# Finer hand-over between dense products and a latency chain in a decoder block: three delays and the place of a yield

## The chip, the cores and the metric

One core of a Trainium2 chip runs one launch of the kernel. The metric is the device time of that launch in microseconds: 951.49 us as the median of three runs before the change (948.81 to 954.71). A second, profiled execution took 951.66 us; all rows below are from it.

## The reference, cut to what matters

A decoder block on 512 tokens of 1024 channels. One normed input feeds one wide projection; its columns go to two branches, which a gate merges, and a feed-forward part follows.

```
xn = rms_norm(h, mix_norm);  proj = xn @ w_in
# attention branch: 8 heads of 64; a small "indexer" picks 128 keys for each query
scores = sum_h relu(q_idx[h] . k_idx / 8) * w_idx[h];  sel = top_k(scores, 128)
y_attn = softmax(rms(q) . rms(k)[sel] / 8 + rel_bias) @ v[sel]
# recurrent branch (RWKV-7): a linear recurrence over time with 8 states of 64 x 64
state = state * d_t + (state @ -kk_t) b_t + v_t k_t ;  y_t = state @ r_t
y = group_norm(y) * ln_w + ln_b + sum(r * k * r_k) * v     # the last term: the "bonus"
merged = sigmoid(gate_attn) * (y_attn @ w_a) + sigmoid(gate_rwkv) * (y_rwkv @ w_r)
h = h + merged @ w_out
h = h + (silu(hn @ w_gate) * (hn @ w_up)) @ w_down,   hn = rms_norm(h, ffn_norm)
```

All tensors are float32.

## The kernel before, in words

**Dense products.** Every weight product is split: a weight chunk is rounded to a high part (`w_hi`, ScalarE, L239) and the rest is a low part (`w_lo`, GpSimd, or VectorE for every third chunk, L243); activations are split in the same way. Three TensorE products, hi by hi, hi by lo and lo by hi, make one step of the sum (`dense_t`, L255 to L264). These are the tiles `ps_d` of the profile. They wait for little, and there is always a next one, until the program's own list of them is at a point that needs a branch's result.

**Chains.** Between the dense products the kernel puts the latency-bound work: index scores (`scores`), the choice of 128 keys by 16 rounds of max and match-replace on VectorE (`select`), head norms (`queries`, `keys`, `key_norms`, each asking TensorE for sums of squares by `head_sums`), attention (`attention`, 4 query tiles by 8 heads, in units of one head: flip the weights of the head two units back, logits of this head, values of the head three back), the operands of the recurrence (`prepare`, `operands`, with a small product for the bonus, L714), the triangular inverses of its four 128-token tiles (`invert`), its eight chunk steps (`steps`) and `head_norm`.

**What sets the order.** TensorE's order is written out while the program is built, by the class `Streams`: each piece of work is a generator with a rank, and a clock `now` that adds an assumed time for each product. At every `yield` the generator says how long after now it wants to go on (or which signal it waits for), and the piece of the lowest rank that is due goes next; the dense products have the highest rank number and fill what is left. The delays stand in the table `L` (L89). Nothing on the chip looks at that clock: the order is fixed, and where a delay was too short TensorE, which works in order, stands and waits. VectorE, ScalarE, GpSimd and the DMA queue of SyncE get their order from a scheduler that follows TensorE's.

The pieces and delays that the change touches: `dense_t` yields once for three products; `L["sums"]` stands between a square of a head tile on ScalarE and its sum on TensorE (L489, L512, L687); `L["attn"]` has one delay for each query tile, after each attention unit (L550); `L["bonus"]` stands between the GpSimd product `ag` (L709) and its sum on TensorE (L719). The point where the dense list needs the recurrence is `yield "yr"` (L1045): the products of `yr` follow it.

Of the kernel before, what the change touches and what calls it, by code (L numbers as in the profile page):

```python
# [82 lines left out]
for _n, _c in _PARS:  # L83
# [2 lines left out]

L = dict(norm=3.0, normed=1.3, score=0.4, pick=0.15, rms=6.5, sums=2.5, attn=(1.0, 0.6, 0.4, 0.35), attn_out=2.0, sig=0.3,  # L89
         prep=5.0, oper=6.0, bonus=6.0, mat=0.5, mats=2.8, inv_u=3.25, inv_t=1.4, inv_r=1.4, inv_n=0.9, inv_e=1.8,  # L90
         inv=1.8, vals=0.6, st_b=1.0, st_u=1.36, st_m=1.4, hn_b=4.55, hn_n=6.55, hn_g=2.0)
POOL_ONLY = 17
COPIES = 23
# [34 lines left out]
def hybrid_block(ctx: ExitStack, tc: tile.TileContext, x, first, rows, consts, lora, rel_bias, stream, out):  # L128
# [10 lines left out]
    def bank(tag, dt=F32, name=None):  # L139
        n = {"d": 3, "i": 2, "c": 3}[tag]  # L140
        return pp.tile([128, 512], dt, name=name or "ps_" + tag, tag=tag, bufs=n)
# [19 lines left out]
    def mm(o, w, r, **kw):  # L161
        nc.tensor.matmul(o, w, r, **kw)  # L162
        n = 1
        for d in r.shape[1:]:
            n *= d
        st.now += max(n * 4 / 2400, 0.107) if r.dtype == F32 else max(n / 2400, 0.03)
# [51 lines left out]
    def cst(name):  # L218
        o, e = CONST_AT[name]
        return con[:, o:e]  # L220
# [34 lines left out]
    def dense_t(ps, wt, c, act, t0=0, t1=S):  # L255

        k = len(act)
        for j in range(k):
            xh, xl = act[j][0][:, t0:t1], act[j][1][:, t0:t1]
            hi, lo = wt[j][0][:, c], wt[j][1][:, c]  # L260
            mm(ps, hi, xh, start=(j == 0), stop=False)
            mm(ps, hi, xl, start=False, stop=False)
            mm(ps, lo, xh, start=False, stop=(j == k - 1))
            yield 0.0  # L264

# [36 lines left out]
    def dense_halves(outs, act, name):  # L302

        for t in (0, 2):
            yield f"{name}{t}"
            yield f"{name}{t + 1}"
            for ps, wt in outs:
                yield from dense_t(ps[:, t * 128:t * 128 + 256], wt, slice(0, 128), act, t * 128, t * 128 + 256)
# [6 lines left out]
    def norm(t, src, gain, to, name):  # L315
# [11 lines left out]
        for g in range(2):  # L327
            nc.vector.scalar_tensor_tensor(xs[g], src[g], ss[:, 3:4], gain[g], op0=OP.mult, op1=OP.mult)
        yield L["norm"]
        ts = slice(t * 128, t * 128 + 128)  # L330
        for g in range(2):
# [4 lines left out]
            nc.vector.tensor_sub(to[1][g][:, :, ts], ps, to[0][g][:, :, ts])  # L336
        st.signal(f"{name}{t}", L["normed"])

# [70 lines left out]
    def scores():  # L409
        for i in range(1, NT):  # L410
            n = (i + 1) * 128
            sc = unit("score")[:, :n]
            for h in range(H):
# [7 lines left out]
                else:  # L421
                    r = unit("relu")[:, :n]
                    nc.scalar.activation(r, ps, AF.Relu)
                    nc.vector.scalar_tensor_tensor(sc, r, w, sc, op0=OP.mult, op1=OP.add)  # L424
                yield L["score"]
            nc.vector.tensor_add(sc[:, n - 128:], sc[:, n - 128:], cst("causal"))
# [3 lines left out]
    def select():  # L430
        for i in range(1, NT):
            yield f"score{i}"
            sc, n = keep[i], (i + 1) * 128
            for _ in range(TOPK // 8):
                m8 = small("max8", 8)
                nc.vector.max(m8, sc)  # L436
                nc.vector.match_replace(sc, m8, sc, TAKEN)  # L437
                yield n / 480 + L["pick"]
            nc.vector.tensor_scalar(sc, sc, CUT, NEG, op0=OP.is_gt, op1=OP.mult)
# [32 lines left out]
    def queries(j, ps):  # L472
# [5 lines left out]
        def rest():  # L478
            s = head_sums(sq)
            nc.vector.tensor_scalar(qss[:, :, 2 * j:2 * j + 2], s.rearrange("q (t h) -> q t h", h=2), RMS_EPS, None,  # L480
                                    op0=OP.add)
            if j == 3:
                flat = lambda q: q.rearrange("q t h -> q (t h)")
                nc.gpsimd.tensor_tensor(flat(qrs[:, 0]), flat(qss), half, op=OP.pow)
                nc.vector.tensor_mul(flat(qrs[:, 1]), flat(qss), flat(qrs[:, 0]))
                st.signal("q", 8.0)
            yield 0.0

        st.add(3, rest(), L["sums"])  # L489

    def keys(j, ps):
# [4 lines left out]
        def rest():  # L496
# [4 lines left out]
            nc.scalar.activation(hv(sq), rs[:, :, None].to_broadcast([128, 8, 64]), AF.Copy)  # L501
            yield L["rms"]
            ps = bank("i")
# [458 lines left out]
    def gate(dst):  # L962

        ps = bank("d")
        yield from dense_t(ps, w_tile(128), slice(0, 128), xn)
        nc.scalar.activation(dst, ps, AF.Tanh, scale=0.5)

    def gated(dst, j, wt, act):
        ps = bank("d")
        yield from dense_t(ps, wt, slice((j % 2) * 128, (j % 2) * 128 + 128), act)  # L970
        nc.vector.scalar_tensor_tensor(dst, dst, 1.0, ps, op0=OP.add, op1=OP.mult)
# [239 lines left out]
```

## Time and profile before

| what | value |
|---|---|
| median of three runs | 951.49 us |
| profiled execution | 951.66 us |
| its span, first to last instruction | 949.9 us |
| TensorE matmuls (PE) busy | 911.4 us, 96% |
| VectorE (DVE) | 406.5 us, 43% |
| ScalarE (ACT) | 344.5 us, 36% |
| GpSimd (POOL) | 365.4 us, 38% |

The chain that ended last is 79% TensorE and 11% VectorE by share of the span. The VectorE share is an average: the profile's 40 slices show it at 8 to 9 tenths in the third to eighth slice and at 1 tenth or less from the 26th on, where the feed-forward part runs on TensorE alone.

### The profile page before, as it was taken

Reading aid. Unit: us, or ns where it says so; the run is one execution under the profiler, and the core shown is the slowest. Engines: PE = TensorE matmul, PEld = TensorE weight load, DVE = VectorE, ACT = ScalarE, POOL = GpSimd, SP = SyncE. Lnnn points to the kernel's source line nnn. Section 1 sums busy time; section 2 is a strip of 40 time slices with the busy share of each in tenths; the row PEclk is TensorE's granted clock in tenths of the full one; section 3 lists DMA queues with packets and bytes.
Section 4 is the critical chain, followed back from the end, with each engine's and each line's share of the span. In section 5 each row is a group of like instructions: output and inputs, shape, how many; then the busy total and the mean of one; then the engine's idle time right before and its main releaser. Section 6 shows DMA issues by size and latency. Waiting matters only on the chain.

```text
span 949.9 us, 13573 instructions
## 1 busy us (share of the span) xinstructions
PE 911.4 (96%) x5526; PEld 765.4 (81%) x5526; DVE 406.5 (43%) x796; ACT 344.5 (36%) x548; POOL 365.4 (38%) x242
## 2 busy tenths in 40 slices
PE   7999899899989999999998999999999999999998
PEld 5988797688767777878886998888888888888886
DVE  4389898873573546573534616111111111100111
ACT  5554565543542433233423324323223232221120
POOL 6425532203264353525415632443534344432321
PEclk9999899999999999999999999999999999999999
DMA  6321232101222120201142332233232332332431
GB/s 230 92 79 44 88 117 68 45 1 59 86 67 67 46 67 23 68 20 50 46 133 79 94 94 68 89 94 106 88 111 89 99 101 90 91 108 89 138 107 44
DMA packets 24173, 77.77 MB, mean 82 GB/s; under 512 B 2869, under 2 KB 4366, under 8 KB 24112
## 3 DMA queue, kind: packets, MB, share of 16 engines
q1 hardware_dynamic: 20688, 72.49, 24.3%
q10 hardware_dynamic: 3424, 4.43, 1.7%
q8 instruction: 43, 0.70, 0.3%
q14 instruction: 18, 0.15, 0.0%
HBM read 74.53 MB, written 2.38 MB: 81 GB/s over the span
## 4 chain that ended last, share of the span: by engine, by line
PE 79%; DVE 11%; ACT 3%; POOL 3%; issue 3%; DMA 1%; SPq 0%; ACTq 0%; POOLq 0%; DVEq 0%
PE ps_d L162 57%; PE ps_c L162 11%; PE ps_i L162 9%; DVE score L437 2%; DVE max L436 2%; PE ps_c L169 2%; DVE score L424 1%; POOL w_lo L243 1%; DMA xa<-in_x_dram 1%; DVE qs L460 1%; PE ps_i L169 1%; ACT w_hi L239 1%; ACT lg L574 0%; POOL bb L700 0%; DVE w_lo L243 0%
## 5 line engine op out<-in xcount | busy, mean ns | idle before, releaser
L243 POOL TENSOR_TENSOR w_lo<-w_raw,w_hi 128x1024 fp32r<-128x1024 f32 (+1 forms) x94 | 221.1, 2354 | 366.8 <-ACT w_hi L239 360.0
L239 ACT ACTIVATE w_hi<-w_raw 128x1024 fp32r<-128x1024 f32 x129 | 136.6, 1060 | 370.9 <-PE ps_d L162 213.1
L162 PE MATMUL ps_d<-xnh,w_hi 128*128 128x512 f32 (+2 forms) x360 | 149.7, 416 | 0.0
L162 PE MATMUL ps_d<-hnl,w_hi 128*128 128x512 f32 (+1 forms) x368 | 139.9, 380 | 0.4 <-DVE hnl L336 0.4
L162 PE MATMUL ps_d<-hnh,w_hi 128*128 128x512 f32 (+1 forms) x368 | 139.9, 380 | 0.0
L162 PE MATMUL ps_d<-hnh,w_lo 128*128 128x512 f32 (+1 forms) x368 | 139.7, 380 | 0.0
L162 PE MATMUL ps_d<-xnh,w_lo 128*128 128x512 f32 (+2 forms) x360 | 137.6, 382 | 0.0
L162 PE MATMUL ps_d<-xnl,w_hi 128*128 128x512 f32 (+2 forms) x360 | 137.4, 382 | 0.0
L243 DVE TENSOR_TENSOR w_lo<-w_raw,w_hi 128x1024 fp32r<-128x1024 f32 x37 | 45.6, 1233 | 130.8 <-ACT w_hi L239 130.0
L1095 DVE TENSOR_TENSOR gsig<-ps_d,gsig 128x512 f32<-128x512 f32 x22 | 15.2, 692 | 157.6 <-PE ps_d L162 156.9
L162 PEld LDWEIGHTS ps_d<-hnl,w_hi 128*128 128x128 f32 x368 | 69.2, 188 | 13.8 <-DVE hnl L336 0.6
L162 PEld LDWEIGHTS ps_d<-hnh,w_lo 128*128 128x128 f32 x368 | 69.2, 188 | 13.1
L162 PEld LDWEIGHTS ps_d<-hnh,w_hi 128*128 128x128 f32 x368 | 69.2, 188 | 13.0
L162 PEld LDWEIGHTS ps_d<-xnh,w_lo 128*128 128x128 f32 x360 | 68.9, 191 | 13.1
L162 PEld LDWEIGHTS ps_d<-xnh,w_hi 128*128 128x128 f32 x360 | 69.4, 193 | 11.7 <-issue 2.6
L162 PEld LDWEIGHTS ps_d<-xnl,w_hi 128*128 128x128 f32 x360 | 69.4, 193 | 9.9 <-issue 1.9
L1099 POOL TENSOR_TENSOR ul<-gsig,uh 128x512 fp32r<-128x512 f32 x22 | 31.6, 1434 | 25.3 <-ACT uh L1098 25.3
L801 POOL COPY rr<-eye 128x512 f16<-128x512 f16 x20 | 13.5, 680 | 57.2 <-PE ps_i L162 57.2
L162 PE MATMUL ps_d<-w_hi,mh 128*128 128x256 f32 x120 | 34.0, 284 | 0.0
L162 PE MATMUL ps_d<-w_hi,ml 128*128 128x256 f32 x120 | 34.0, 283 | 0.0
L162 PE MATMUL ps_d<-w_lo,mh 128*128 128x256 f32 x120 | 34.0, 283 | 0.0
L574 ACT ACTIVATE lg<-lg,mx,qrs 128x128 f32<-128x128 f32 (+3 forms) x32 | 20.8, 649 | 22.1 <-DVE mx L573 22.0
(291 smaller groups left out, 1698.5 us busy)
## 6 DMA issues: line engine op xcount, KB each, us to landing
w_raw<-in_stream_dram SPq DMA_DIRECT2D x129, 512.0 KB, 3.6
xa<-in_x_dram SPq DMA_DIRECT2D x4, 512.0 KB, 5.8
ht<-in_x_dram ACTq DMA_DIRECT2D x8, 256.0 KB, 3.1
out_dram<-ht SPq DMA_DIRECT2D x8, 256.0 KB, 2.2
toep<-bias_table ACTq DMA_DIRECT2D x8, 128.0 KB, 3.4
gain<-in_rows_dram ACTq DMA_DIRECT2D x2, 256.0 KB, 3.1
con<-in_consts_dram SPq DMA_DIRECT2D x1, 321.0 KB, 6.9
bias_table<-tab ACTq DMA_DIRECT2D x1, 276.0 KB
```

The costliest lines, as they stand in the source:

```text
L162: nc.tensor.matmul(o, w, r, **kw)
L169: nc.tensor.transpose(o, src, idn)
L239: nc.scalar.activation(hi, raw, AF.Copy)
L243: eng.tensor_sub(lo[:, o:o + n_], raw[:, o:o + n_], hi[:, o:o + n_])
L424: nc.vector.scalar_tensor_tensor(sc, r, w, sc, op0=OP.mult, op1=OP.add)
L436: nc.vector.max(m8, sc)
L437: nc.vector.match_replace(sc, m8, sc, TAKEN)
L460: nc.vector.scalar_tensor_tensor(lo[b, h], src[a], gain[a], hi[a, h], op0=OP.mult, op1=OP.subtract)
L574: nc.scalar.activation(lg, lg, AF.Exp, scale=scale, bias=mx[:, 2:3], accum_out=den[:, h:h + 1])
L801: nc.gpsimd.tensor_copy(two(R, 1), eye16.rearrange("q (g w s) -> q g w s", w=2, s=s)[:, None, :, 1] .to_broadcast([128, H, 64 // s, s]))
L1095: nc.vector.tensor_mul(g, pu, g)
L1099: nc.gpsimd.tensor_sub(ul, g, uh)
```

## The change

Three numbers or groups of numbers in the table of delays change, and `dense_t` gives way behind each product instead of behind each third. `dense_k` and `dense_tiles`, the other two forms of dense product, are as before. Two lines are added to the file, so all lines behind L261 have a number higher by two in the new kernel.

```diff
-L = dict(norm=3.0, normed=1.3, score=0.4, pick=0.15, rms=6.5, sums=2.5, attn=(1.0, 0.6, 0.4, 0.35), attn_out=2.0, sig=0.3,
-         prep=5.0, oper=6.0, bonus=6.0, mat=0.5, mats=2.8, inv_u=3.25, inv_t=1.4, inv_r=1.4, inv_n=0.9, inv_e=1.8,
+L = dict(norm=3.0, normed=1.3, score=0.4, pick=0.15, rms=6.5, sums=4.0, attn=(0.9, 0.9, 0.95, 1.0), attn_out=2.0, sig=0.3,
+         prep=5.0, oper=6.0, bonus=9.0, mat=0.5, mats=2.8, inv_u=3.25, inv_t=1.4, inv_r=1.4, inv_n=0.9, inv_e=1.8,
...
             mm(ps, hi, xh, start=(j == 0), stop=False)
+            yield 0.0
             mm(ps, hi, xl, start=False, stop=False)
+            yield 0.0
             mm(ps, lo, xh, start=False, stop=(j == k - 1))
             yield 0.0
```

What it does to the order, at three places.

ScalarE, at the squares of the key tiles (`ksq<-ps_d` is the square of a tile, `ksq<-qrs` the spread of an earlier tile's norm, `kh<-kraw` the scaled keys of that earlier tile). Before:

```order
L493 ACTIVATE ksq<-ps_d 128x512
L494 ACTIVATE kraw<-ps_d,fst 128x512
L501 ACTIVATE ksq<-qrs 128x512 x2
L456 ACTIVATE kh<-kraw 64x512
L462 ACTIVATE kh<-kraw 64x512
L456 ACTIVATE kh<-kraw 64x512
L462 ACTIVATE kh<-kraw 64x512
L493 ACTIVATE ksq<-ps_d 128x512
L494 ACTIVATE kraw<-ps_d,fst 128x512
```

Now:

```order
L495 ACTIVATE ksq<-ps_d 128x512
L496 ACTIVATE kraw<-ps_d,fst 128x512
L503 ACTIVATE ksq<-qrs 128x512
L495 ACTIVATE ksq<-ps_d 128x512
L496 ACTIVATE kraw<-ps_d,fst 128x512
L503 ACTIVATE ksq<-qrs 128x512
L458 ACTIVATE kh<-kraw 64x512
L464 ACTIVATE kh<-kraw 64x512
L458 ACTIVATE kh<-kraw 64x512
L464 ACTIVATE kh<-kraw 64x512
```

The third tile's square stood behind two spreads and four scalings; it stands behind one spread now.

TensorE, in the attention of the last query tile (`lg` are the weights to flip, `kh` and `kl` the logits, `vt` the values, `ps_d` the dense products). Before:

```order
L162 MATMUL ps_c<-kh,qs 128x512
L162 MATMUL ps_c<-kl,qs 128x512
L162 MATMUL ps_i<-vt,pt 128x64 x4
L162 MATMUL ps_d<-xnh,w_hi 128x512
L162 MATMUL ps_d<-xnl,w_hi 128x512
L162 MATMUL ps_d<-xnh,w_lo 128x512
L169 MATMUL ps_c<-fst,lg 128x128 x4
L162 MATMUL ps_c<-kh,qs 128x512
L162 MATMUL ps_c<-kl,qs 128x512
L162 MATMUL ps_i<-vt,pt 128x64 x4
L169 MATMUL ps_c<-fst,ytile 128x128 x4
L169 MATMUL ps_c<-fst,lg 128x128 x4
```

Now:

```order
L162 MATMUL ps_c<-kh,qs 128x512
L162 MATMUL ps_c<-kl,qs 128x512
L162 MATMUL ps_i<-vt,pt 128x64 x4
L162 MATMUL ps_d<-xnl,w_hi 128x512
L162 MATMUL ps_d<-xnh,w_lo 128x512
L162 MATMUL ps_d<-xnh,w_hi 128x512
L162 MATMUL ps_d<-xnl,w_hi 128x512
L162 MATMUL ps_d<-xnh,w_lo 128x512
L169 MATMUL ps_c<-fst,lg 128x128 x4
L162 MATMUL ps_c<-kh,qs 128x512
L162 MATMUL ps_c<-kl,qs 128x512
L162 MATMUL ps_i<-vt,pt 128x64 x4
```

Between two units stand five dense products where three, or none, stood.

TensorE, where the dense list comes to `yr` (`zg` and `z_g` are the last head norm's products). Before:

```order
L169 MATMUL ps_d<-fst,ytok 128x128 x4
L162 MATMUL ps_d<-zg,g2a 128x128
L162 MATMUL ps_d<-z_g_128,g2b 128x128
L162 MATMUL ps_d<-zg,g2a 128x128
L162 MATMUL ps_d<-z_g_128,g2b 128x128
L162 MATMUL ps_d<-zg,g2a 128x128
L162 MATMUL ps_d<-z_g_128,g2b 128x128
L162 MATMUL ps_d<-zg,g2a 128x128
L162 MATMUL ps_d<-z_g_128,g2b 128x128
L162 MATMUL ps_d<-yr,w_hi 128x512 x2
```

Now, up to the first seven of the 60 dense products that follow:

```order
L162 MATMUL ps_d<-zg,g2a 128x128
L162 MATMUL ps_d<-z_g_128,g2b 128x128
L162 MATMUL ps_d<-zg,g2a 128x128
L162 MATMUL ps_d<-z_g_128,g2b 128x128
L162 MATMUL ps_d<-xnh,w_hi 128x512
L162 MATMUL ps_d<-xnl,w_hi 128x512
L162 MATMUL ps_d<-xnh,w_lo 128x512
L162 MATMUL ps_d<-xnh,w_hi 128x512
L162 MATMUL ps_d<-xnl,w_hi 128x512
L162 MATMUL ps_d<-xnh,w_lo 128x512
L162 MATMUL ps_d<-xnh,w_hi 128x512
```

Sixty dense products of 512 columns stand between the last head norm and the first product of `yr`, where none stood.

## Rows read from the trace of the kernel before

**Rows 1.** Busy time by stage: busy us (instructions) of each engine, granted clock, DMA.
```profile
50.00:145.00 95.00, 88.21 (x508) 77.84 (x508) 87.33 (x202) 53.63 (x88) 38.64 (x16) 0.95 0.26 79
145.00:222.00 77.00, 70.04 (x446) 59.09 (x445) 59.73 (x200) 41.66 (x97) 12.05 (x6) 0.98 0.14 44
```

**Rows 2.** TensorE's waits: tile and line, releaser, us in total, times, longest.
```profile
PE ps_c L169 <- ACT lg L574: 7.7, 10, 1.7
PE ps_i L162 <- POOL ag L709: 5.0, 3, 2.8
...
PE ps_i L162 <- ACT ksq L493: 4.3, 1, 4.3
PE ps_d L162 <- ACT yr L1048: 3.5, 1, 3.5
...
PE ps_i L162 <- ACT tt L811: 1.8, 2, 0.9
PE ps_i L162 <- DVE uu L814: 1.6, 2, 0.8
PE ps_c L162 <- DVE score L420: 1.1, 1, 1.1
```

**Rows 3.** Windows of 5 us around the lower clock (PEclk stands before DMA).
```profile
105.00:110.00 5.00, 2.67 (x10) 2.54 (x11) 4.08 (x11) 4.86 (x8) 0.38 (x1) 0.56 0.00 0
110.00:115.00 5.00, 5.00 (x25) 4.25 (x23) 3.88 (x10) 3.62 (x7) 3.60 (x2) 0.76 0.12 14
200.00:205.00 5.00, 5.00 (x26) 4.32 (x24) 3.08 (x9) 1.56 (x4) 0.80 (x1) 0.66 0.01 2
510.00:515.00 5.00, 4.78 (x13) 3.60 (x14) 2.50 (x5) 1.48 (x3) 0.00 (x0) 0.68 0.05 17
```

**Rows 4.** ScalarE's timeline at the keys: start, us, instruction, idle before.
```profile
103.58 0.63 ACT L501 ACTIVATE ksq<-qrs 128x512 f32<-128x512 f32 x1 [5.56 <-POOL qrs L500]
...
106.71 0.57 ACT L493 ACTIVATE ksq<-ps_d 128x512 f32<-128x512 f32 x1
```

**Rows 5.** Timelines of TensorE and VectorE at the first attention unit.
```profile
140.09 0.22 PE L162 MATMUL ps_c<-kh,qs 128*128 128x128 f32 x1
...
144.82 0.33 PE L169 MATMUL ps_c<-fst,lg 128*128 128x128 f32 x1 [1.38 <-ACT lg L574]
...
142.24 0.33 DVE L563 SCALAR_TENSOR_TENSOR lg<-toep,qrs,ps_c 128x128 f32<-128x128 f32 x1
...
143.34 0.68 DVE L436 MAX8 max<-score 128x8 f32<-128x512 f32 x1
```

**Rows 6.** TensorE's timeline behind a foreign product (head sums): three dense starts.
```profile
90.43 0.49 PE L162 MATMUL ps_d<-xnh,w_hi 128*128 128x512 f32 x1
90.75 0.40 PE L162 MATMUL ps_d<-xnl,w_hi 128*128 128x512 f32 x1
90.99 0.40 PE L162 MATMUL ps_d<-xnh,w_lo 128*128 128x512 f32 x1
```

**Rows 7.** GpSimd's timeline at the third bonus product.
```profile
276.43 2.37 POOL L243 TENSOR_TENSOR w_lo<-w_raw,w_hi 128x1024 fp32r<-128x1024 f32 x1 [1.25 <-ACT w_hi L239]
278.76 1.70 POOL L709 TENSOR_TENSOR ag<-zr,ag 128x512 f32<-128x512 f32 x1
```

**Rows 8.** TensorE and ScalarE timelines inside an inverse.
```profile
376.70 1.06 ACT L239 ACTIVATE w_hi<-w_raw 128x1024 fp32r<-128x1024 f32 x1 [1.30 <-PE ps_d L162]
...
382.29 0.41 PE L162 MATMUL ps_i<-rr,uu 128*128 128x64 f16 x8
...
382.80 0.60 ACT L811 ACTIVATE tt<-ps_i 128x512 f16<-128x512 f32 x1 [4.01 <-PE ps_i L162]
```

**Rows 9.** VectorE and GpSimd timelines in the index scores.
```profile
58.49 2.17 DVE L424 SCALAR_TENSOR_TENSOR score<-relu,widx,score 128x384 f32<-128x384 f32 x1
...
61.85 0.59 DVE L424 SCALAR_TENSOR_TENSOR score<-relu,widx,score 128x384 f32<-128x384 f32 x1
...
57.85 2.40 POOL L243 TENSOR_TENSOR w_lo<-w_raw,w_hi 128x1024 fp32r<-128x1024 f32 x1 [9.74 <-ACT w_hi L239]
```

## The prediction

> **What bounds the kernel now.** I read TensorE's waits first, then the busy time by stage, then the timelines around each long wait. TensorE is busy nearly all the time, so the change can only earn the stalls, and what the lower clock costs behind them. The waits [rows 2] say where the stalls are: 7.7 us in ten waits of the attention's flips for the exponentials (`lg`), 5.0 us in three waits of the bonus sums for GpSimd (`ag`), 4.3 us in one wait for the square of a key tile (`ksq`), 3.5 us in one wait for `yr`. The rest of these rows, 4.5 us, are waits that no edit aims at. The windows [rows 3] show the price behind a stall: the granted clock falls from its upper level (2.4 GHz) towards the lower (1.2 GHz) behind the `ksq` wait (0.56 and 0.76), in the attention (0.66) and behind the `yr` wait (0.68). As busy time times the missing share this is 2.67 x 0.44 + 5.00 x 0.24 = 2.4 us, 5.00 x 0.34 = 1.7 us and 4.78 x 0.32 = 1.5 us.
>
> The stages [rows 1] say which wait ends last. From 50 to 145 us VectorE is busy for 87.33 of 95 us, hardly less than TensorE with 88.21: it scores and picks the keys. There TensorE is not alone in setting the pace. From 145 to 222 us VectorE is busy for 59.73 of 77 us and has room.
>
> **The change, part by part.** The sum is made against the profiled execution's 951.66 us, which lies 0.2 us above the median.
>
> *Sums of squares, asked for 1.5 us later.* The 4.3 us wait is one of queueing: ScalarE had the square of the third key tile behind the spread of the second tile's norm and four scalings, idled 5.56 us for GpSimd in front of that spread and reached the square at 106.71 us [rows 4]. In the new order the square stands ahead of them, so this wait goes: 4.3 us and 2.4 us of clock, 6.7 us for TensorE alone. But TensorE then comes 6.7 us sooner to the first attention unit, and there VectorE is late already: the first logits are issued at 140.09 us, VectorE takes them at 142.24 us, between rounds of picking of which one max alone takes 0.68 us, and the flip waits 1.38 us [rows 5]. VectorE's picking is the same work as before. It can come earlier only by idle time that the stall itself made, and in the stage it has 95 - 87.33 = 7.7 us of that in all [rows 1]. So the gain lies between nothing (VectorE no earlier) and 6.7 us. I take 3.0, a little under the middle, since at 92% busy VectorE has little to give.
>
> *Even delays in the attention.* For the first query tile a unit gets five dense products where it had six; for the last two tiles five where it had three or none. A weight row has two units to become ready, so its cover grows by some 2 x 2 x 0.23 = 0.9 us in the late units and shrinks by 2 x 0.23 = 0.5 us in the first tile (0.23 to 0.24 us from one dense start to the next [rows 6]). Of the 7.7 us, 1.38 belong to the first flip; 6.3 remain in nine waits, none over 1.7 us. Taking 0.9 us from each leaves about 1 us. With the 1.7 us of clock and 1.0 us lost again in the first tile's units the gain is 6.3 - 1.0 + 1.7 - 1.0 = 6.0 us. Bounds: 2 (VectorE sets the pace here too) and 8.0.
>
> *Bonus sums, asked for 3 us later.* The longest of the three waits is 2.8 us [rows 2], so 3 us would cover each. GpSimd does the product in order, with a weight rest of 2.37 us just ahead of the third one [rows 7], and such a rest stands ahead of two of the four in the new order as well. I leave 0.7 us of the 5.0: gain 4.3, bounds 1 and 5. Nobody waits for a later bonus before the first head norm asks for it (L931).
>
> *Finer yields.* A request that is due is now served behind the running product instead of up to two products later. Over all the requests in a row the whole recurrence comes earlier against the dense list, although the attention is stretched: 60 dense products, 60 x 0.23 = 13.8 us, stand behind the last head norm, where none stood. The 3.5 us wait for `yr` and its 1.5 us of clock go, with 0.2 us of a second wait there: 5.2 us, bounds 4.5 and 5.5.
>
> *What the finer yields cost.* First, changes of kind: behind a foreign product the next dense start comes after 0.32 us instead of 0.24 [rows 6]. The dense products stand in 194 unbroken runs in the new order, in 173 before: 21 x 0.08 = 1.7 us. The Trainium skill, "TensorE: Matmul & The Clock Gate", section "Step-by-step: what each phase is for", has the next weights loading while the running product streams, so that products follow each other at their column count, whatever they are. By that rule these 1.7 us would be nothing and the sum below 1.7 us lower; the row disagrees, and the row is used.
>
> Second, thinner cover in the recurrence. There the dense products between a result and its use fall from 9 to 7 and from 6 to 5, by 0.45 and 0.23 us. An inverse's result is ready 0.60 us after ScalarE or VectorE takes it, 0.7 us behind its last product [rows 8], and five dense products with the foreign product ahead cover 1.4 us. So most uses lose slack only. Where a weight rounding of 1.06 us stands ahead on ScalarE [rows 8] the result takes some 1.7 us and TensorE waits 0.3. Of some 60 such uses I let six wait: 1.7 us, bounds 0 and 10 (half of the 60 at 0.33). The index scores get two dense products a head instead of three; the 1.1 us wait there [rows 2] is left as it is.
>
> Third, the longer wait that I expect at the first flips can bring the lower clock there: 1.0 us, bounds 0 and 2.4, as behind the `ksq` wait.
>
> *Sum:* 3.0 + 6.0 + 4.3 + 5.2 = 18.5 us off, 1.7 + 1.7 + 1.0 = 4.4 us on: 951.66 - 14.1 = **937.5 us**.
>
> **Rivals.**
>
> *A. Every stall aimed at goes.* The first stage gives its whole 6.7 us, the attention 8.0, the bonus 5.0, `yr` 5.2, and only the 1.7 us for changes of kind is paid: 951.66 - 24.9 + 1.7 = 928.5 us. For it: each wait has a cover longer than itself in the new order. Against it: VectorE at 92% [rows 1].
>
> *B. The wait moves to VectorE and GpSimd.* The first stage gives nothing, the attention 2 (its waits are VectorE's queue, not TensorE's haste), the bonus 2 because GpSimd is as late as it is asked; `yr` gives 5.2, and 3.4 us are paid for changes of kind and cover: 951.66 - 9.2 + 3.4 = 945.9 us. For it: TensorE reaches the first flip earlier than VectorE can serve it [rows 5]. Against it: from 145 us VectorE has 17 us of room [rows 1].
>
> *C. Slower: the recurrence loses its cover.* One mechanism: VectorE's evictions there hold up TensorE when GpSimd runs beside them. A score operation of VectorE took 2.17 us while a GpSimd rest of 2.40 us ran, and 0.59 us in the clear [rows 9], so a collision costs 1.6 us and brings a result of 0.7 us to 2.3 us. Nine dense products cover 2.1 us and let 0.2 us show; seven cover 1.6 us and five 1.4 us with the foreign product, so 0.7 to 0.9 us shows. The point from which it decides: 14.1 us must be lost at 0.8 us each, so 18 of the 60 uses must collide; at 25 the time is 937.5 + 20 = 957.5 us. The Trainium skill, "SBUF — State Buffer", section "SBUF: two separate sides", says that a VectorE operation with two SBUF inputs and a GpSimd operation hold a shared port in turn, each for its whole length. The row of 2.17 us agrees. Against the rival: evictions in the recurrence mostly read PSUM, and TensorE's waits for `tt` and `uu` are 3.4 us in all before [rows 2].
>
> That the edits do nothing is no rival: the order shows them in place.
>
> **How the numbers follow.** Forecast 0.55 (own range 930 to 944), A 0.17, B 0.22, C 0.06. The range 927 to 949 takes in A's centre and B with 3 us of GpSimd's waits on top, and leaves out the far ends of A and B and all of C, about 2 in 10. A measurement of this kernel tells about 1% from no change: faster means under 942.0 us. That holds for 0.85 of the forecast, all of A and a tenth of B: 0.47 + 0.17 + 0.02 = 0.66. Slower means over 961 us, the far half of C: 0.03. The rest, 0.31, is the same within 1%.
>
> **What would show it.** In the changed kernel's waits `ksq` and `yr` should be gone and `ag` under 1.5 us; the `lg` waits should sum to 4 to 7 us, with the first flip's the longest, 3 to 5 us, and those past 160 us at 2 us or less. The clock should be full around 105 and 510 us. From 50 us to the first attention unit VectorE should be over 94% busy. Waits for `tt`, `uu`, `rr` and `vu` should total 3 to 6 us. Wrong would be: a first flip that waits no longer than before (A), `lg` or `ag` waits as long as now (B), or over 15 us of waits in the recurrence (C).

## The result, and the profile after

The changed kernel takes 940.27 us (median of four runs, 937.07 to 943.17), the kernel before 951.88 us beside it: ratio 0.9878, 95% interval 0.9833 to 0.9922, 11.6 us less. Its profiled execution took 937.07 us (span 934.9 us) and is the lowest of the four; against the profiled 951.66 us that is 14.6 us less. The forecast was 937.5 us (951.66 - 14.1 is 937.56).

TensorE's waits in the changed kernel (tile and line, releaser, us in total, times, longest), beside [rows 2]:

```profile
PE ps_c L169 <- ACT lg L576: 6.2, 6, 2.3
...
PE ps_i L169 <- ACT ksq L503: 2.2, 1, 2.2
PE ps_c L162 <- DVE score L422: 1.9, 1, 1.9
PE ps_i L162 <- DVE uu L816: 1.8, 2, 1.1
PE ps_i L162 <- ACT tt L813: 1.6, 2, 1.1
```

`ag` and `yr` have left the list, 8.5 us together. The `ksq` wait is another one now: not for the square of a tile but for the spread of a norm (L503, the flip of `ksq`). `lg` has fallen only from 7.7 to 6.2 us.

Busy time by stage and around the places of the lower clock (PEclk is the column before the DMA share), beside [rows 1, 3]:

```profile
50.00:145.00 95.00, 88.50 (x517) 77.52 (x516) 90.82 (x214) 53.75 (x92) 38.78 (x16) 0.97 0.27 83
105.00:110.00 5.00, 5.00 (x38) 4.65 (x37) 4.82 (x12) 4.87 (x8) 2.31 (x1) 1.00 0.05 13
142.00:147.00 5.00, 4.92 (x21) 3.65 (x20) 4.40 (x14) 2.04 (x6) 0.00 (x0) 0.66 0.06 25
145.00:222.00 77.00, 73.00 (x466) 62.84 (x466) 58.95 (x190) 41.67 (x96) 16.10 (x8) 0.99 0.15 45
510.00:515.00 5.00, 5.00 (x24) 4.14 (x23) 4.03 (x4) 2.12 (x4) 4.88 (x4) 1.00 0.22 53
...
387.00:396.00 9.00, 7.94 (x82) 7.43 (x81) 5.40 (x9) 3.76 (x7) 3.83 (x5) 0.81 0.01 3
```

The clock is full at 105 and 510 us, and lower in two new places, behind the first flip and in the recurrence. VectorE is busy for 90.82 of 95 us up to 145 us, where it was 87.33.

### The profile page after: what moved, and what is told of

Read it like the earlier page. It is cut to its first block, busy times and chain, and to the rows that moved or that the text cites. A ratio compares the mean times of both kernels' runs of the same rounds, so it can differ in the third digit from the quotient of the medians.

```text
span 934.9 us, 13570 instructions
## 1 busy us (share of the span) xinstructions
PE 906.9 (97%) x5526; PEld 763.2 (82%) x5526; DVE 412.5 (44%) x796; ACT 344.0 (37%) x548; POOL 363.7 (39%) x242
## 4 chain that ended last, share of the span: by engine, by line
PE 84%; DVE 11%; issue 2%; ACT 2%; POOL 1%; DMA 1%; SPq 0%; DVEq 0%; ACTq 0%; POOLq 0%
PE ps_d L162 60%; PE ps_c L162 11%; PE ps_i L162 9%; DVE score L439 2%; DVE max L438 2%; PE ps_c L169 2%; DVE kl L459 1%; POOL w_lo L243 1%; DMA xa<-in_x_dram 1%; DVE score L426 1%; DVE lg L569 0%; PE ps_i L169 0%; DVE w_lo L243 0%; ACT lg L576 0%; PE ps_d L169 0%
## 5 line engine op out<-in xcount | busy, mean ns | idle before, releaser
L243 POOL TENSOR_TENSOR w_lo<-w_raw,w_hi 128x1024 fp32r<-128x1024 f32 (+1 forms) x94 | 223.5, 2379 | 355.0 <-ACT w_hi L239 328.8
L162 PE MATMUL ps_d<-xnl,w_hi 128*128 128x512 f32 (+2 forms) x360 | 141.8, 394 | 0.0
L162 PE MATMUL ps_d<-xnh,w_hi 128*128 128x512 f32 (+2 forms) x360 | 141.4, 393 | 0.0
L162 PE MATMUL ps_d<-xnh,w_lo 128*128 128x512 f32 (+2 forms) x360 | 141.0, 392 | 0.0
L243 DVE TENSOR_TENSOR w_lo<-w_raw,w_hi 128x1024 fp32r<-128x1024 f32 x37 | 47.5, 1283 | 127.2 <-ACT w_hi L239 126.7
L162 PEld LDWEIGHTS ps_d<-xnh,w_hi 128*128 128x128 f32 x360 | 68.7, 191 | 11.7 <-issue 1.0
L438 DVE MAX8 max<-score 128x8 f32<-128x256 f32 (+2 forms) x48 | 26.7, 559 | 1.0
```

What stands on the lines that cost most here:

```text
L243: eng.tensor_sub(lo[:, o:o + n_], raw[:, o:o + n_], hi[:, o:o + n_])
```

## Where the time came from

I split a span in three: TensorE's waits from the start of the span to its last instruction (the 4.6 us before its first product among them), the loss by the clock (span times one minus the mean granted clock), and the rest, which is TensorE's own work and 3.8 us behind its last instruction. Before: 949.9 = 34.6 + 9.5 (clock 0.990) + 905.8. Changed: 934.9 = 24.1 + 5.6 (0.994) + 905.2. So 10.5 us are waits, 3.9 us clock, and TensorE's own work has not changed.

The table has all kernels tried. "Early waits" are TensorE's waits between 50 and 146 us, at the scores, the keys and the first flips; clock and waits are those of the profiled execution. "At full clock" is the median, over the runs, of span times mean granted clock: an estimate of the span without the loss by the clock, good to half a microsecond in one run since the clock has three decimals. The kernels ran in four batches, each beside its own runs of the kernel before (medians 951.9, 954.1, 953.6 and 955.0 us), so medians of different batches do not compare; the ratios do, and the full-clock figures: the kernel before has 940.4, 940.6 and 940.4 us in the last three.

| kernel | median us | ratio to before (95%) | at full clock | early waits | all waits | clock |
|---|---|---|---|---|---|---|
| before | 951.9 | | 940.4 | 6.8 | 34.6 | 0.990 |
| changed | 940.3 | 0.9878 (0.9833 to 0.9922) | 929.3 | 6.4 | 24.1 | 0.994 |
| sums alone | 952.8 | 0.9992 (0.9968 to 1.0015) | 940.7 | 6.7 | 35.3 | 0.990 |
| attention alone | 949.0 | 0.9945 (0.9921 to 0.9969) | 933.9 | 6.7 | 29.4 | 0.988 |
| bonus alone | 950.7 | 0.9958 (0.9932 to 0.9984) | 935.0 | 6.8 | 31.0 | 0.985 |
| finer yields alone | 948.4 | 0.9937 (0.9909 to 0.9964) | 937.8 | 6.8 | 30.2 | 0.989 |
| all but finer yields | 940.7 | 0.9857 (0.9835 to 0.9878) | 929.4 | 5.2 | 24.1 | 0.989 |
| changed, six a unit | 930.9 | 0.9766 (0.9740 to 0.9792) | 925.0 | 6.4 | 21.0 | 0.998 |
| changed, later spread | 939.1 | 0.9837 (0.9815 to 0.9859) | 927.1 | 6.2 | 23.5 | 0.989 |
| changed, half the picks | 931.5 | 0.9755 (0.9733 to 0.9777) | 924.7 | 4.1 | 21.4 | 0.996 |
| before, half the picks | 953.5 | 0.9975 (0.9952 to 0.9999) | 938.4 | 6.0 | 33.6 | 0.985 |
| sums alone, half the picks | 950.4 | 0.9948 (0.9920 to 0.9975) | 935.8 | 2.6 | 30.0 | 0.994 |
| six a unit, `kl` on GpSimd | 927.3 | 0.9715 (0.9686 to 0.9744) | 925.0 | 5.8 | 19.9 | 1.000 |
| the same, later spread | 926.0 | 0.9697 (0.9667 to 0.9728) | 922.3 | 3.6 | 17.4 | 0.998 |

## The experiments

**The four parts, each alone on the kernel before.**

```diff
-sums=2.5
+sums=4.0
```

> The kernel before with one part of the change: the sums of squares are asked for 1.5 us later, nothing else. Theory S (the parts pay separately, each in its own place): the 4.3 us wait for the key square goes, and the lower clock behind it; TensorE comes sooner to the first attention unit, where the flip's wait grows from 1.4 to 3 to 5 us; the time falls by 3 us (0 to 6.7). Rival T (the parts need each other: a request is only served on time with the finer yields): the key square's wait shrinks to 1 to 2 us, the time falls by under 2 us. Rival V (VectorE alone sets the end of this stage): the wait goes, the first flip waits 4 us more than before, and the time does not change.

The time did not change (ratio 0.9992). TensorE's waits from 50 to 146 us in this kernel:

```profile
PE ps_i L169 <- ACT ksq L501: 2.2, 1, 2.2
PE ps_c L162 <- DVE score L420: 2.1, 1, 2.1
PE ps_d L162 <- POOL w_lo L243: 1.2, 1, 1.2
PE ps_c L169 <- ACT lg L574: 1.2, 1, 1.2
```

The 4.3 us wait for the square is gone and 6.7 us of waits stand there all the same, where 6.8 stood. Rival V had the time right and the place wrong: the first flip waits no longer than before; the stall is spread over the scores, a weight rest and the spread of the norm. The lower clock moved too, in the profiled executions. From 50 to 142 us the clock is 0.98 where it was 0.94, and TensorE comes to the first flip at 142.2 us for 144.8, with the same products ahead of it; but from 270 to 285 us the clock is 0.77 where it was full, and the span is no shorter (951.0 us).

```diff
-attn=(1.0, 0.6, 0.4, 0.35)
+attn=(0.9, 0.9, 0.95, 1.0)
```

> The kernel before with one part of the change: even delays between the attention's units, nothing else. Theory S: the lg waits past the first flip fall from 6.3 us to 1 to 3 us, the lower clock at 201 us goes, the time falls by 4 to 6 us; the bonus and yr waits stay at 5.0 and 3.5 us. Rival T (the finer yields did the rest): the lg waits stay above 4 us and the time falls by 2 us or less.

Theory S holds: `lg` waits in four places instead of ten, of which the first flip has 1.28 us, and the time falls by 5.2 us by the ratio. TensorE's waits here and the stage of the attention:

```profile
PE ps_i L162 <- POOL ag L709: 5.0, 3, 2.8
...
PE ps_c L169 <- ACT lg L574: 1.9, 4, 1.3
```

```profile
145.00:222.00 77.00, 75.45 (x469) 64.29 (x468) 61.33 (x197) 42.52 (x96) 18.50 (x9) 1.00 0.16 49
```

TensorE is busy for 75.45 of 77 us there, with 70.04 before [rows 1] and 73.00 in the changed kernel. In this stage the same delays did more alone than within the change.

```diff
-bonus=6.0
+bonus=9.0
```

> The kernel before with one part of the change: the bonus sums are asked for 3 us later, nothing else. Theory S: the three ag waits, 5.0 us, fall to under 0.7 us, the time falls by 4.3 to 5 us; all other waits stay as they are. Rival B (GpSimd is as late as it is asked, or the wait moves to the next user): half of the 5.0 us stays in ag or shows at another tile, the time falls by 2 us or less.

One `ag` wait of 1.2 us is left of three with 5.0, and the time falls by 4.0 us by the ratio; nothing new waits. Theory S, a little under its size.

```diff
             mm(ps, hi, xh, start=(j == 0), stop=False)
+            yield 0.0
             mm(ps, hi, xl, start=False, stop=False)
+            yield 0.0
```

> The kernel before with one part of the change: a request may be served behind every dense product, not behind every third; all delays are those of before. Theory S: the yr wait of 3.5 us and its lower clock at 511 us go (5.2 us); the ksq, lg and ag waits stay within 1.5 us of before; the waits in the recurrence (uu, tt, rr, vu) stay within 3 to 6 us; changes of kind cost 1 to 2 us; the time falls by 2 to 4 us. Rival T (the finer service carries the change): lg and ag waits fall to half as well, and the time falls by 8 us or more. Rival C (thinner cover): waits in the recurrence rise over 6 us and the time falls by under 1 us or rises.

The time falls by 6.0 us by the ratio, more than theory S had and less than rival T; at full clock it falls by 2.6 us, within theory S's 2 to 4. The waits:

```profile
PE ps_c L169 <- ACT lg L576: 9.5, 11, 1.9
...
PE ps_i L162 <- POOL ag L711: 2.5, 2, 1.6
...
PE ps_i L162 <- ACT ksq L495: 2.0, 2, 1.3
```

`yr` is gone, and `ag` and `ksq` have halved too, because the requests fall elsewhere in the row. Against that `lg` rises from 7.7 to 9.5 us: with service behind every product a unit gets the products that its delay says, not the next multiple of three.

**Do the parts add up?** Alone they gave 0.8, 5.2, 4.0 and 6.0 us, 16.0 together; the change gave 11.6. At full clock it is -0.3, 6.5, 5.4 and 2.6 us, 14.2 together, and 11.1 for the change: they overlap by either measure.

```diff
 # the changed kernel
             mm(ps, hi, xh, start=(j == 0), stop=False)
-            yield 0.0
             mm(ps, hi, xl, start=False, stop=False)
-            yield 0.0
```

> The changed kernel without the finer yields: sums, attention and bonus are asked for as in the change, but a request waits for the end of a group of three dense products. The single parts measured 0.8 us (sums), 5.2 (attention), 4.0 (bonus) and 6.0 (finer yields), 16.0 together, the whole change 11.6. Theory O (the parts overlap: with finer yields the bonus already gains 2.5 us and the attention loses cover): this kernel is 9 to 11 us faster than the kernel before, its lg waits are 2 to 3 us against 6.2 in the changed kernel, its yr wait stays at 3.5 us; the finer yields add 1 to 3 us on top of the other parts. Theory S (parts separate, the difference is noise): it is 5 to 6 us faster than before, since the finer yields carry 6.0 of the 11.6.

Theory O, and further than it went: without the finer yields the kernel is 13.6 us faster than before by the ratio, where I had 9 to 11, and no slower than the changed kernel (929.4 and 929.3 us at full clock). What the yields gave at `yr` they took at `lg`:

```profile
PE ps_d L162 <- ACT yr L1048: 3.5, 1, 3.5
PE ps_c L169 <- ACT lg L574: 3.3, 7, 1.9
...
PE ps_i L162 <- POOL ag L709: 1.2, 1, 1.2
```

Against the changed kernel that is 3.5 us more for `yr` and 2.9 less for `lg`; all waits are 24.1 us in both.

```diff
-attn=(0.9, 0.9, 0.95, 1.0)
+attn=(1.15, 1.15, 1.15, 1.15)
```

> The changed kernel with the attention's delays at 1.15 for all four query tiles: six dense products a unit instead of five. Theory O (what is left of the lg waits is cover lost by the finer yields): the lg waits fall from 6.2 to 3 us or less, the first flip's from 2.3 to 1.4, and the time by 3 to 5 us against the changed kernel (ratio to before 0.983 to 0.986). Rival (VectorE sets the pace of the attention): the lg waits stay above 5 us, the time stays within 1 us of the changed kernel.

Theory O again. By the two ratios the time falls by 1.1% against the changed kernel, some 10 us, where I had 3 to 5. At full clock it is 4.3 us (929.3 to 925.0), within the 3 to 5; the rest is clock, with medians of 0.991 and 0.996. The waits, and the stage of the attention:

```profile
PE ps_i L169 <- ACT ksq L503: 3.3, 2, 2.1
...
PE ps_c L169 <- ACT lg L576: 1.6, 5, 0.7
```

```profile
145.00:222.00 77.00, 75.61 (x474) 64.95 (x472) 58.54 (x195) 42.66 (x97) 18.51 (x9) 1.00 0.16 49
```

The profiled spans are 6.4 us apart: the `lg` waits fall by 4.6 us and all waits by 3.1, and the clock gives 3.7 (5.6 us lost at 0.994, 1.9 at 0.998). The first flip's 2.3 us are now 0.3, but `ksq` has 1.1 us more: the early waits are 6.4 us as before.

**What holds the early waits at 6 to 7 us?**

```diff
-rms=6.5
+rms=9.5
```

> The changed kernel with the spread of a key tile's norm flipped 3 us later (delay 9.5 instead of 6.5). Theory Q (the sums' gain went into ScalarE's order: the spread stands behind four scalings of the tile ahead): the 2.2 us wait for ksq goes, the first flip waits 2.3 to 3 us, the time falls by 2 to 3 us against the changed kernel. Rival V (VectorE sets the end of the stage): the ksq wait goes and the first flip's grows to 4 us or more; the time stays within 1 us.

In this kernel the waits from 50 to 146 us are:

```profile
PE ps_c L169 <- ACT lg L576: 4.3, 2, 2.5
PE ps_c L162 <- DVE score L422: 1.9, 1, 1.9
```

The `ksq` wait of 2.2 us is gone, and 2.0 us more stand at the first two flips (2.5 and 1.8 us). The time does not decide: it is 1.2 us lower by the medians, some 4 by the ratios, whose intervals overlap, and 2.2 at full clock, where the runs overlap too. I go by the waits: what left `ksq` came back at the flips, 6.4 us before and 6.2 after, as rival V has it, though its price stood in two flips, not one. Theory Q, which saw the loss in ScalarE's order alone, does not explain the second flip.

```diff
-            for _ in range(TOPK // 8):
+            for _ in range(TOPK // 16):
```

> The changed kernel with half of the picking rounds left out (8 of 16 maxima for each query tile, so other keys are kept). Rival V (VectorE, 95% busy from 50 to 145 us, holds up TensorE in that stage): the ksq and first lg waits, 2.2 and 2.3 us, go, and the time falls by 4 us or more. Theory Q (TensorE waits there for queue order on ScalarE, VectorE's load is not the bound): the ksq wait stays at 1.5 us or more, the first lg wait falls to under 1 us since no picking stands between its steps, the time falls by 1 to 2.5 us.

The early waits are 4.1 us and no flip waits among them; VectorE is busy for 74.13 of 95 us:

```profile
PE ps_c L162 <- DVE score L422: 1.9, 1, 1.9
PE ps_i L169 <- ACT ksq L503: 1.6, 1, 1.6
PE ps_d L162 <- POOL w_lo L243: 0.6, 1, 0.6
```

```profile
50.00:145.00 95.00, 90.93 (x545) 79.95 (x544) 74.13 (x158) 57.13 (x102) 41.33 (x17) 1.00 0.27 82
```

The time is 1.2% below the changed kernel's by the two ratios and 4.6 us at full clock, more than rival V's 4 us by either; yet a `ksq` wait of 1.6 us stays, as theory Q had it. So both limits are there, and I took them apart in the kernel before:

```diff
 # before, and before with sums=4.0
-            for _ in range(TOPK // 8):
+            for _ in range(TOPK // 16):
```

> The kernel before with half of the picking rounds left out (8 of 16 maxima a query tile). Theory V (VectorE sets the pace up to the first attention unit): the wait for the key square, which is one of ScalarE's order, stays near 4 us, the first flip's goes, score and w_lo waits stay; the time falls by 2 to 4 us. Theory Q (VectorE is not the pace, only the order of the queues): the waits to 145 us, 6.8 us, stay within 1 us and the time falls by under 2 us.

> Half of the picking rounds left out, and the sums of squares asked for 1.5 us later, nothing else of the change. To be read against the kernel before with half of the rounds. Theory V: with room on VectorE the sums pay at last, since nothing late stands behind them: the waits to 145 us fall by 2 to 4 us and the time by 3 to 6 us. Theory Q (the gain is lost in ScalarE's order at the spread of the norm, whatever VectorE does): the spread waits 2 us again, the waits to 145 us fall by under 1.5 us and the time by under 2 us.

With room on VectorE alone the time falls by 0.25%, some 2 us, and the early waits only from 6.8 to 6.0 us, within the 1 us of theory Q. The signs of theory V are there as well: the first flip no longer waits, and the square's wait stays at 4.1 us, one of order:

```profile
PE ps_i L162 <- ACT ksq L493: 4.1, 1, 4.1
```

So this run alone does not choose. With the sums as well the early waits fall to 2.6 us:

```profile
PE ps_c L162 <- DVE score L420: 2.1, 1, 2.1
PE ps_i L169 <- ACT ksq L501: 0.5, 1, 0.5
```

Beside each other the two kernels take 953.5 and 950.4 us, 3.0 us for the sums, where they gave nothing with the full picking. At full clock the steps are 940.4, 938.4 and 935.8 us, and 940.7 for the sums alone. The waits fall by 3.4 us, within theory V's 2 to 4, the time by its lower bound. The intervals of the two overlap (0.9952 to 0.9999, 0.9920 to 0.9975), so I rest on the waits and on the full-clock figures (937.6 to 939.5 us in the twelve runs without the sums, 935.0 to 937.9 with them). Leaving rounds out also changes the order of what is left on VectorE; its load and its order are not told apart here.

**The same without leaving work out.**

```diff
 # six a unit
-                nc.vector.tensor_sub(lo[b, h], src[a], hi[a, h])
+                nc.gpsimd.tensor_sub(lo[b, h], src[a], hi[a, h])
```

> The changed kernel with six dense products a unit (delays of 1.15), and the eight subtractions that make the low part of the keys moved from VectorE to GpSimd. They take VectorE 7.4 us between 50 and 145 us, where it is busy for 96%, and GpSimd has some 55 us free there. Theory V: the waits to 145 us fall from 6.4 us to 3 to 5 us, and the time by 1.5 to 4 us against the kernel with six products. Rival (GpSimd is slower and in order, so ScalarE's second scalings and the weight rests come later): a wait for w_lo or ksq of 2 us or more, the time the same or longer.

> As the kernel with the subtractions on GpSimd, and the spread of a key tile's norm flipped 3 us later (9.5). Theory V: with VectorE relieved the ksq wait goes and does not come back at the first flips: the time falls by another 1 to 3 us. Rival: the wait comes back at the first flips as it did in the changed kernel (1.8 and 2.5 us), the time stays within 1 us.

GpSimd takes 1.29 us for a subtraction (VectorE's mean in the kernel with six a unit was 0.92), as the group of this line from 50 to 145 us shows:

```profile
L459 POOL TENSOR_TENSOR kl<-kraw,kh 64x512 fp32r<-64x512 f32 x8 | 10.3, 1286 | 2.2 <-ACT kh L458 1.7
```

The time falls by 0.5% by the ratios, but theory V's early waits of 3 to 5 us are missed: 5.8. VectorE is still busy for 90.58 of 95 us. At full clock this kernel takes 925.0 us, as the one with six a unit does, so no gain at full clock is shown; of the 3.3 us between the two profiled spans 1.1 are waits and some 1.7 clock. Adding the later spread brings early waits of 3.6 us: here the `ksq` wait of 2.8 us does not come back in full (first flip 1.7 us where it had 0.2). At full clock it takes 922.3 us, 2.7 less by the medians, but the six runs without the later spread go from 921.8 to 925.4 us; by the times it is 1.3 us, within theory V's 1 to 3, and the intervals overlap. The gain rests on the waits, 19.9 us in all before and 17.4 after. This is the fastest version, 926.0 us, 0.9697 of the kernel before.

## Why the prediction was right or wrong

**The sum came out, though not by its terms.** The change gave 14.6 us in the profiled execution for 14.1 forecast. The median gain, 11.6 us, is smaller because the profiled execution had the highest clock of the four runs (0.994; the others 0.991, 0.985, 0.991). It stays in the range, and below the 942.0 us that I set for faster. At full clock the change is worth 11.1 us. Put in the forecast's own places, the two profiled executions give 2.8 us (sums, 2.4 of it clock), 4.1 (attention), 5.0 (bonus) and 5.2 (`yr`) off and 3.9 us on. That is 13.2 of the 15.0 us between the spans; the rest lies in small waits and clock elsewhere. So that the total came within 0.5 us is partly luck: what the attention fell short was made up in places that I had not priced.

**Sums, 3.0 us: wrong, near nothing.** In the change the early waits went from 6.8 to 6.4 us, and the 2.4 us of clock around 105 us are mostly lost again behind the first flip (4.92 x 0.34 = 1.7 us). Alone the sums did not change the time (ratio 0.9992); the mean clock was 0.990 in both profiled executions, 0.990 and 0.987 as medians of all runs, and at full clock they gained nothing (940.4 and 940.7 us). The reason I gave (VectorE cannot come earlier) was right in the main and I did not follow it to its end: my lower bound was the answer. VectorE was busy for 90.82 of 95 us, 95.6%, for my "over 94%". I also put the whole return at the first flip, 3 to 5 us. It had 2.3, and 2.2 us came back earlier, at the spread of the norm. There ScalarE's queue and VectorE are both late; timelines of VectorE, GpSimd and ScalarE in the changed kernel:

```profile
117.91 0.16 DVE L501 TENSOR_SCALAR qss<-ps_i 128x8 f32<-128x8 f32 x1
118.15 1.64 POOL L502 TENSOR_TENSOR qrs<-qss,half 128x8 f32<-128x8 f32 x1 [4.11 <-DVE qss L501]
...
119.89 0.61 ACT L458 ACTIVATE kh<-kraw 64x512 fp32r<-64x512 f32 x1
...
121.82 0.63 ACT L464 ACTIVATE kh<-kraw 64x512 fp32r<-64x512 f32 x1
122.47 0.63 ACT L503 ACTIVATE ksq<-qrs 128x512 f32<-128x512 f32 x1
...
123.15 0.66 PE L169 MATMUL ps_i<-fst,ksq 128*128 128x128 f32 x4 [2.21 <-ACT ksq L503]
```

GpSimd has the root by 119.8 us, and the spread runs at 122.47, behind four scalings of 0.6 us of the key tile ahead. It is the order of [rows 4] once more, one instruction further on. Taking that wait away alone moves it to the flips (later spread), and room on VectorE with the sums lets them pay (half the picks).

**Attention, 6.0 us: too large by half.** The `lg` waits past the first flip fell from 6.3 to 3.9 us, 2.4 us, and with the 1.7 us of clock at 201 us the term is about 4. I wrote that 0.9 us off each of nine waits leaves about 1 us. That is what the delays give alone. In the change the finer yields set each unit at five products where groups of three had made six of the same delay; I charged this to the first tile only, at 1.0 us. Six a unit brings all `lg` waits to 1.6 us. The sum of the `lg` waits, 6.2 us, lay within my 4 to 7, but those past 160 us have 3.3 us, not 2 or less.

**Bonus, 4.3 us: right.** All 5.0 us went. Alone the delay took 3.8 us, so 3 us more did not cover every wait as I had it; without the finer yields 1.2 us stay, and they took the rest by shifting the requests.

**Finer yields, 5.2 us at `yr`: right in place,** wait and lower clock both gone. In sum they were worth nothing beside the other three parts with these delays: 929.3 us at full clock with them, 929.4 without.

**Costs, 4.4 us: the size about right, made up otherwise.** The recurrence's waits for `uu`, `tt`, `vu` and `am` are 4.5 us, within my 3 to 6, where 3.8 stood: 0.7 us for my 1.7. The lower clock behind the first flip took 1.7 us for my 1.0 (the 1.7 us set against the sums above, to be counted once), and one in the recurrence, around 392 us, takes 7.94 x 0.19 = 1.5 us that I had not priced. The score wait, which I left at 1.1 us, is 1.9; it is 2.1 both with the sums alone and with the yields alone, so the two dense products a head are not its only cause. The 1.7 us for changes of kind is not to be seen: TensorE's own work is 905.2 us, 905.6 and 904.8 in kernels with finer yields (changed, six a unit, the fastest), 905.8, 906.2 and 905.2 in kernels without (before, sums alone, all but finer yields). It is 907.6 with the yields alone, so an effect of 1 or 2 us hides in the spread, and I leave it open. The price of one change is there. TensorE in the attention of the changed kernel:

```profile
137.74 0.28 PE L162 MATMUL ps_c<-kl,qs 128*128 128x128 f32 x1
137.85 0.45 PE L162 MATMUL ps_d<-xnl,w_hi 128*128 128x512 f32 x1
138.14 0.39 PE L162 MATMUL ps_d<-xnh,w_lo 128*128 128x512 f32 x1
138.37 0.39 PE L162 MATMUL ps_d<-xnh,w_hi 128*128 128x512 f32 x1
```

The dense product behind the foreign one lets the next start after 0.29 us, the one behind it after 0.23, as in [rows 6] with 0.32 and 0.24. By the Trainium skill, "TensorE: Matmul & The Clock Gate", section "Step-by-step: what each phase is for", products that follow each other do so at their column count, and it names no exception for a change of kind; by that the two should be alike. The rows disagree, while the total tells neither.

**Rivals.** A was wrong for the first stage and the attention: the flips still wait for 6.2 us, the first longer than before (2.3 us for 1.38), and the time is 11.7 us above A's 928.5. B was right for the first stage (gain nothing) and wrong for the bonus. Its 2 us for the attention came near the 2.4 us of waits, but not its reason: six products a unit took the `lg` waits to 1.6 us, so VectorE's queue did not hold them. C did not come: the recurrence waits for 4.5 us, not for over 15. In the keys one VectorE subtraction took 2.23 us beside a GpSimd weight rest, 0.69 us in the clear, but that is not the recurrence:

```profile
116.53 0.69 DVE L459 TENSOR_TENSOR kl<-kraw,kh 64x512 fp32r<-64x512 f32 x1
...
120.73 2.23 DVE L459 TENSOR_TENSOR kl<-kraw,kh 64x512 fp32r<-64x512 f32 x1
...
120.06 2.35 POOL L243 TENSOR_TENSOR w_lo<-w_raw,w_hi 128x1024 fp32r<-128x1024 f32 x1 [0.28 <-ACT w_hi L239]
```

It ends only after the rest does, as the Trainium skill, "SBUF — State Buffer", section "SBUF: two separate sides", has it for a VectorE operation with two SBUF inputs.

## What to carry to other kernels

Where a second engine is nearly always busy in a stage (here VectorE with 92 to 96%), do not count a removed wait in it: sum the waits of the whole stage before and after, and count on a gain only if that engine gets room too. When the grain of a schedule changes, read every delay again in whole units of the new grain; here a delay of 0.9 us meant six products before and five after, and six products again were worth 4.3 us at full clock, beside 11.1 for the whole change. Weigh edits together where one alone shows nothing: the sums and the room on VectorE paid little or nothing singly.

## What the runs showed that I had not expected

The time at full clock repeats about twice as well as the time. In 23 runs of the kernel before, the times go from 952.02 us at a mean granted clock of 0.989 to 960.99 us at 0.978; span times clock stays within 937.7 to 941.7 us. The four kernels with 21.4 us of waits or less have a median clock of 0.996 to 0.998, the ten with 23.5 us or more 0.985 to 0.991, in no order of their waits. What sets it in a single run is not shown. The medians are 0.987 before and 0.998 in the fastest. Of the 29.0 us between their medians (954.98 and 925.98 us) some 10.6 us are clock, 953.2 x 0.013 = 12.4 less 924 x 0.002 = 1.8. I had priced the clock from the 5-us windows of one execution, at 1.5 to 2.4 us a place.
